# Tokens on partitions for values, gates and branch products: 512 weight columns a product, weight parts in pairs

## The chip, the core and the metric

The kernel runs on one core of a Trainium2 chip, in one launch. The metric is the device time in microseconds. The engines are named as the profile names them: PE (matrix products), PEld (its weight loads), ACT, DVE, POOL, and SP, which here only issues DMAs. The program is built with a scheduler: the code gives the instructions a priority, and the scheduler puts them into one fixed order for each engine. Each engine then runs its queue in that order, and an instruction that waits holds up all that stand behind it.

## The reference, cut to what matters

Two layers, 256 tokens, 1024 features, float32. `_mixer` projects the normalized input onto the columns of `w_in`, runs two recurrences on parts of them, and merges the two results under gates; `_conv_ffn` follows.

```python
x = x + W_out( sig(h Wg_dn) * (DeltaNet_bi(h) W_dn) + sig(h Wg_hg) * (HGRN2_bi(h) W_hg) ),  h = RMSNorm(x)
x = x + ConvGLU(RMSNorm(x))

p = h @ w_in
(qkv, z, beta_r, a_r, hq, hf_fwd, hf_bwd, hi, hgate, gate_dn, gate_hg) = _split(p, IN_SIZES)
...
o_dn = _gated_rmsnorm(o_dn, z...)          # o * rsqrt(mean(o^2)) * w * silu(z)
o_hg = _gated_rmsnorm(o_hg, hgate...)
merged = (jax.nn.sigmoid(gate_dn) * (o_dn @ w_branch_dn)
          + jax.nn.sigmoid(gate_hg) * (o_hg @ w_branch_hg))
return merged @ w_out
...
gate = _dwconv(gate, ffn_conv) + ffn_conv_bias
return (jax.nn.silu(gate) * up) @ w_down
```

## The kernel before, in words

**Products.** Most matrix products are made three times over in the type fp32r. A weight piece (128 x 1024 values: four blocks of 128 rows by 256 columns) arrives by DMA as `raw`; ACT casts it to `wh`, DVE subtracts to get the remainder `wl`; the activations have parts `xh` and `xl` in the same way. A product is then `wh*xh + wh*xl + wl*xh`, summed in a PSUM bank (`Gemm`, lines 208 to 244). The pools hold three `raw`, three `wh` and three `wl` (each one piece). Some projections skip the split and multiply plain float32 (`gemm32`, line 249): numbers 1, 4, 5, 6 and 14 of `w_in`, and 2 and 3 ahead of the mixer (`Pre`).

**Layout.** Nearly every product has a 128 x 128 block of weights as the stationary operand and 256 tokens as the moving one, so the result has channels on partitions. For z, the HGRN2 gate (projections 14 to 17, `silu_gate`) and the HGRN2 values (9 and 13, `hi_`) it is turned round with `tokens=True`: a 128 x 128 block of activations is stationary, and 256 weight columns move. The gates (18 to 25, `gates`) and the branch products (`branches`, line 913) keep channels on partitions.

**A mixer.** After its first projections it builds the DeltaNet system (`gram`, `solve`, `inverse`, `delta`) and the two HGRN2 halves (`hgrn`, two heads at a time, result `poh`). Then `out_norm` normalizes each half's output: `ob` (copy), `junk` (squares on ACT), `rr` (root), `on` on DVE, four or two transposes `pto` on PE, and `ohl`, the two parts, on ACT and DVE. `branches` multiplies `ohl` by the branch weights (bank `pbr`), multiplies by the sigmoid gates `sgt`, adds the two branches (`mg`) and splits the sum into `mhi` and `mlo`; `project` multiplies those by `w_out`. The gate projections depend on nothing late, so they stand in PE's queue beside the chains of the recurrences.

**Order.** The strings `"order"` in `OPT`, one for each layer, list the stages (`k0` conv, `z0` gate, `hi0` values, `g0` gates, `hg1` HGRN2, `ho1` its output, `br`, `pr`) with a priority offset each; weight splits stand 2000 ahead of their users (`"ahead"`). The feed-forward part (`ffn`, line 975) is a loop over 22 blocks of 256 columns of `w_up`, and four column blocks of `w_down`.

Of the kernel before, what the change touches and what calls it, by code (L numbers as in the profile page):

```python
# [17 lines left out]
P = 128  # L18
T = 256
# [9 lines left out]
    "f32": ((1, 4, 5, 6, 14), (1, 4, 5, 6, 14)),  # L29
# [6 lines left out]
    "w": 3,  # L36
    "rp": 20000,
    "eu": 0,
# [5 lines left out]
    "es": ((), ()),  # L44
    "ec": 1,
    "eo": 0,
# [13 lines left out]
    "tmz": 1,  # L60
# [15 lines left out]
# columns of the per-layer vector pack (one value per partition each)  # L76
# [11 lines left out]
# columns of the constants  # L88
# [28 lines left out]
def trunk(ctx: ExitStack, tc: tile.TileContext, x_in, consts, masks, vec, rows, w16, w_in, w_br, w_out, w_up, w_down, out):  # L117
# [21 lines left out]
    class Group:  # L139
        """Matmuls accumulating in one PSUM bank, kept in order; one start, one stop."""  # L140
# [9 lines left out]
    # ---------------------------------------------------------------- constants  # L150
# [32 lines left out]
    # ---------------------------------------------------------------- helpers  # L183
# [8 lines left out]
    def split_piece(src, n):  # L192
        with tc.high_priority(offset=OPT["ahead"]):
            return split_piece_(src, n)

    def split_piece_(src, n, pool=None, bufs=0):
        raw = piece(src, n)
        if pool:
            wh = pool.tile([P, 1024], F32R, tag="eh", name="wh", bufs=bufs)
            wl = pool.tile([P, 1024], F32R, tag="el", name="wl", bufs=bufs)  # L200
        else:
            wh = wp.tile([P, 1024], F32R, tag="wh", name="wh", bufs=OPT["w"])
            wl = wp.tile([P, 1024], F32R, tag="wl", name="wl", bufs=OPT["w"])
        act.copy(wh[:, :n], raw[:, :n])  # L204
        dve.tensor_tensor(wl[:, :n], raw[:, :n], wh.bitcast(F32)[:, :n], ALU.subtract)  # L205
        return (wh[:, :n].rearrange("p (k c) -> p k c", c=256), wl[:, :n].rearrange("p (k c) -> p k c", c=256))

    class Gemm:
        """src[i]: [P, k, 256] pieces; fills a bank: two column tiles (T layout) or two token tiles."""

        def __init__(self, src, xh, xl, nk=KT, tokens=False, tail=0, parts=None):
            self.tail, self.parts = tail, parts
            self.src, self.xh, self.xl, self.nk, self.tokens = src, xh, xl, nk, tokens
            self.ps = pg.tile([P, 512], F32, tag="g", name="ps", bufs=OPT["g"])
            self.g = Group(nk * 6)
            self.k = 0

        def run(self, k1=None):
            nk = k1 or self.nk
            while self.k < nk:  # L220
                last = self.nk - self.k <= 4 * self.tail
                end = nk if last else min(self.k + 4, nk)
                w = []
                for k0 in range(self.k, end, 4):
                    kn = min(4, end - k0)
# [20 lines left out]
    def gemm(src, xh, xl, nk=KT, tokens=False, tail=0, parts=None):  # L246
        return Gemm(src, xh, xl, nk, tokens, tail, parts).run()
# [950 lines left out]
```

## Time and profile before

| what | value |
|---|---|
| median of three runs | 928.67 us (927.70 to 929.71) |
| span of the profiled execution | 926.8 us, 1.9 us under the median, which lies around the span |
| PE busy | 906.6 us, 98% of the span, 7450 instructions |
| DVE busy | 668.5 us, 72% |
| ACT busy | 559.0 us, 60% |
| DMA | 150.07 MB, mean 162 GB/s |
| granted TensorE clock | 0.998 in the mean |

The page's 40 slices are 23.2 us each. The mixer of layer 0 fills the first eleven, its feed-forward part the next nine; layer 1 repeats this from about 470 us. The profile times one execution; its span runs from the first to the last instruction, and the device time has the start and end of the launch on top. In the timeline a row with `x4` stands for four instructions in a row, and starts of neighbouring rows show the pace of PE better than the durations, because products overlap in the array.

### The profile page before, as it was taken

The page shows a single profiled execution, that of the slowest core. Times are in us where ns is not written, and L with a number is a line of the kernel's source. Part 1 is how long each engine was busy: PE and PEld are TensorE (multiplying, and loading weights), DVE is VectorE, ACT ScalarE, POOL GpSimd, SP SyncE. Part 2 cuts the span into 40 slices and gives each one's busy share as a digit, 9 for nine tenths or more (in the row PEclk, how much of TensorE's full clock was granted, in tenths as well). Part 3 has the DMA queues.
Part 4 walks back from the last instruction along what each step waited for, and adds up shares of the span by engine and source line. Part 5 has one row for each costly group of instructions (what it writes and reads, how often), then busy time and mean ns, then how long its engine had stood idle before and what let it go on. Part 6 is the DMA issues. An engine that isn't in the chain of part 4 may idle for free.

```text
span 926.8 us, 18732 instructions
## 1 busy us (share of the span) xinstructions
PE 906.6 (98%) x7450; PEld 887.8 (96%) x7450; DVE 668.5 (72%) x1279; ACT 559.0 (60%) x974; POOL 13.9 (2%) x123
## 2 busy tenths in 40 slices
PE   7999999999999999999999999999999999999997
PEld 6988999999999999999989899999999999999996
DVE  4667997655877888865447889885667788888543
ACT  4698647678566555543437856665855665555443
POOL 0000000000000000000000000000000000000000
PEclk9999999999999999999999999999999999999999
DMA  6455554225567655555505564533265656555552
GB/s 207 137 189 169 171 184 124 69 74 177 183 202 250 186 183 183 183 176 174 171 27 170 183 205 149 152 100 92 91 197 175 192 184 187 183 183 183 171 183 80
DMA packets 51111, 150.07 MB, mean 162 GB/s; under 512 B 13488, under 2 KB 14032, under 8 KB 50768
## 3 DMA queue, kind: packets, MB, share of 16 engines
q1 hardware_dynamic: 50304, 147.96, 50.5%
q8 instruction: 58, 0.95, 0.4%
q10 hardware_dynamic: 720, 0.92, 0.3%
q14 instruction: 29, 0.24, 0.1%
HBM read 146.75 MB, written 2.11 MB: 161 GB/s over the span
## 4 chain that ended last, share of the span: by engine, by line
PE 88%; ACT 4%; DMA 3%; DVE 3%; issue 1%; SPq 0%; DVEq 0%; ACTq 0%
PE ps L146 72%; PE pbr L146 5%; PE pa L830 3%; DMA raw<-in_w_in_dram 2%; DVE wl L205 1%; DMA ld<-dg 1%; PE po L146 1%; PE poh L146 1%; PE psb L146 1%; ACT wh L204 1%; PE ss L146 0%; PE pz L666 0%; PE pr L689 0%; DMA xs<-in_consts_dram 0%; DVE pr L627 0%
## 5 line engine op out<-in xcount | busy, mean ns | idle before, releaser
L204 ACT CAST wh<-raw 128x1024 fp32r<-128x1024 f32 x244 | 251.8, 1035 | 250.7 <-PE ps L146 96.0
L205 DVE TENSOR_TENSOR wl<-raw,wh 128x1024 fp32r<-128x1024 f32 x244 | 293.6, 1205 | 127.1 <-ACT wh L204 123.7
L146 PE MATMUL ps<-xh,wl 128*128 128x256 f32 x1152 | 327.2, 285 | 1.5 <-DVE wl L205 1.5
L146 PE MATMUL ps<-xh,wh 128*128 128x256 f32 x1152 | 327.1, 285 | 1.2 <-ACT wh L204 1.2
L146 PE MATMUL ps<-xl,wh 128*128 128x256 f32 x1152 | 326.2, 284 | 0.0
L146 PEld LDWEIGHTS ps<-xh,wl 128*128 128x128 f32 x1152 | 220.1, 192 | 2.3 <-DVE wl L205 2.1
L146 PEld LDWEIGHTS ps<-xh,wh 128*128 128x128 f32 x1152 | 220.3, 192 | 1.7 <-ACT wh L204 1.4
L146 PEld LDWEIGHTS ps<-xl,wh 128*128 128x128 f32 x1152 | 220.3, 192 | 0.1
L146 PE MATMUL ps<-hl,wh 128*128 128x256 f32 x352 | 99.0, 281 | 0.0
L146 PE MATMUL ps<-hh,wl 128*128 128x256 f32 x352 | 99.0, 281 | 0.0
L146 PE MATMUL ps<-hh,wh 128*128 128x256 f32 x352 | 98.6, 280 | 0.0
L146 PEld LDWEIGHTS ps<-hh,wl 128*128 128x128 f32 x352 | 66.3, 188 | 0.1
L146 PEld LDWEIGHTS ps<-hl,wh 128*128 128x128 f32 x352 | 66.3, 188 | 0.1
L146 PEld LDWEIGHTS ps<-hh,wh 128*128 128x128 f32 x352 | 66.3, 188 | 0.0
L146 PE MATMUL ps<-xnt,raw 128*128 128x256 f32 x256 | 58.8, 380 | 0.0
L146 PEld LDWEIGHTS ps<-xnt,raw 128*128 128x128 f32 x256 | 47.0, 190 | 6.0
L146 PE MATMUL ps<-wl,xh 128*128 128x256 f32 x160 | 47.1, 294 | 0.7 <-DVE wl L205 0.6
L146 PE MATMUL ps<-wh,xh 128*128 128x256 f32 x160 | 46.6, 292 | 0.2 <-ACT wh L204 0.2
L146 PE MATMUL ps<-wh,xl 128*128 128x256 f32 x160 | 46.1, 288 | 0.0
L1001 DVE SCALAR_TENSOR_TENSOR cv<-fpad,vecs,cv 128x256 f32<-128x256 f32 x88 | 42.2, 480 | 4.3
L146 PE MATMUL pbr<-ohl,wh 128*128 128x256 f32 x256 | 45.3, 280 | 0.0
L146 PEld LDWEIGHTS pbr<-ohl,wh 128*128 128x128 f32 x256 | 38.8, 188 | 0.0
(274 smaller groups left out, 1438.1 us busy)
## 6 DMA issues: line engine op xcount, KB each, us to landing
raw<-in_w_in_dram SPq DMA_DIRECT2D x99, 512.0 KB, 3.6
raw<-in_w_up_dram SPq DMA_DIRECT2D x88, 512.0 KB, 3.7
raw<-in_w_down_dram SPq DMA_DIRECT2D x40, 512.0 KB, 3.6
raw<-in_w_br_dram SPq DMA_DIRECT2D x16, 512.0 KB, 3.9
raw<-in_w_out_dram SPq DMA_DIRECT2D x16, 512.0 KB, 4.2
cb<-cd SPq DMA_DIRECT2D x2, 1024.0 KB, 5.6
early<-in_w_in_dram SPq DMA_DIRECT2D x4, 512.0 KB, 7.2
raw<-in_w_down_dram SPq DMA_DIRECT2D x8, 256.0 KB, 3.3
```

The source lines that it names most:

```text
L146: self.prev = chain(pe.matmul(o, lhsT, rhs, start=self.i == 0, stop=self.i == self.n - 1), self.prev)
L204: act.copy(wh[:, :n], raw[:, :n])
L205: dve.tensor_tensor(wl[:, :n], raw[:, :n], wh.bitcast(F32)[:, :n], ALU.subtract)
L830: pe.matmul(pa[:, u // 2, u % 2], kc[:, u * P:(u + 1) * P], view(qa[:, 0, u * P:u * P + 1], [[2 * h, 64 // h], [512 + h, 2], [1, h]]), sta ...
L1001: dve.scalar_tensor_tensor(cv, pad[:, i:i + T], w[:, i:i + 1], cv, op0=ALU.mult, op1=ALU.add)
```

## The change: what it does

1. **Tokens on partitions, 512 columns.** A new `gemm_tok` makes products with a 128 x 128 block of activations stationary and 512 weight columns moving (two pieces side by side, 256 columns of each), into two banks `pst`, one for each block of 128 tokens. z and the HGRN2 gate, the values, the gates and the branch products all use it.
2. **Pairs.** `split_pair` brings two pieces into one tile `w2`, which holds both parts of both; there are two such tiles, where there were three `wh` and three `wl`. All other split products, the feed-forward part's too, take their weights from pairs.
3. **Projection 14** is no longer plain float32.
4. **Merge.** The gated branch results are summed as [token, 512 columns]; PE transposes the sum (`ptm`, four blocks of 128 columns each), and the two parts are split out of that bank into `mg2`, whose first half lies in the buffer `xw` and whose second in `cb`. For each layer there are 8 multiplications and 4 additions of 512 columns, 16 transposes and 4 splits of 512, in place of 8 multiplications of 512, 8 additions and 8 splits of 256.
5. **Names and order.** `qk` lies in the buffer `xw`. The order strings join stages (`hi0` and `hi1` to `hi`, `z0` to `z3` to two, `g0` to `g7` to four) and keep the offsets. Options that were off are removed.

```diff
-    "f32": ((1, 4, 5, 6, 14), (1, 4, 5, 6, 14)),
+    "f32": ((1, 4, 5, 6), (1, 4, 5, 6)),
...
-    "w": 3,
+    "w": 2,
...
-        "g0-5000 hf1-1000 hb1-300 hg1-2000 z2-2000 z3-1000 do-300 g1-300 ho0-1000 g2-3000 ho1 g3 g4-1000 "
-        "g5-1000 g6-9000 g7 br-9000 pr-1000",
+        "g0-5000 hf1-1000 hb1-300 hg1-2000 z1-2000 do-300 g1-300 ho0-1000 g2-3000 ho1 g3 br-9000 pr-1000",
...
-    def split_piece(src, n):
+    def split_pair(srcs, ns=(1024, 1024)):
+
         with tc.high_priority(offset=OPT["ahead"]):
...
+            w2 = wp.tile([P, 2, 2, 1024], F32R, tag="w2", name="w2", bufs=OPT["w"])
+            for i, (src, n) in enumerate(zip(srcs, ns)):
+                raw = piece(src, n)
+                split_act(raw[:, :n], w2[:, 0, i, :n], w2[:, 1, i, :n])
+            return w2
...
+    def gemm_tok(src, xh, xl):
+
+
+        n = len(xh)
+        ps = [pg.tile([P, 512], F32, tag="g", name="pst", bufs=OPT["g"]) for _ in range(2)]
+        gs = [Group(3 * n) for _ in range(2)]
+        for i in range(n // 4):
+            w2 = split_pair([src(i, j) for j in range(2)])
+            for b in range(2):
+                o = ps[b].rearrange("p (j c) -> p j c", j=2)
+                for k in range(4):
+                    wh, wl = (w2[:, e, :, 256 * k:256 * k + 256] for e in range(2))
+                    a, a_ = (t_[4 * i + k][:, b * P:(b + 1) * P] for t_ in (xh, xl))
+                    gs[b].mm(o, a, wh)
+                    gs[b].mm(o, a, wl)
+                    gs[b].mm(o, a_, wh)
+        return ps
...
-            qk = mp.tile([P, 2, H, T], F32, tag="qk", name="qk")
+            qk = xp.tile([P, 2, H, T], F32, tag="xw", name="qk")
...
             def gates(c):
-                j, t0 = divmod(c, 4)
+                j, t0 = divmod(c, 2)
...
+                for b, ps in enumerate(win_tok(18 + 2 * c)):
+                    act.activation(sgs[0][:, b, j, 512 * t0:512 * t0 + 512], ps, AF.Sigmoid)
...
+            def silu_gate(i):
+                sz.append(mp.tile([P, 2, 512], F32, tag=("t1", "ke")[i], name="sz"))
+                for b, ps in enumerate(win_tok(14 + 2 * i)):
...
+            def hi_():
+                iv = late().tile([P, 2, 512], F32, tag="iv", name="iv")
+                for b, ps in enumerate(win_tok(9, 13)):
+                    act.copy(iv[:, b], ps)
...
+                for c in range(2):
+                    m_ = (xp, mp)[c].tile([P, 2, 4, T], F32R, tag=("xw", "cb")[c], name="mg2")
+                    tms = []
                     for i in range(2):
...
+                        for b, ps in enumerate(gemm_tok(lambda _, j: w_br[l, 2 * c + j, i], oh[i], ol[i])):
+                            tm = tmp("mg", ("tmp", "tmh")[i])
+                            dve.tensor_tensor(tm, ps, sgs[0][:, b, i, 512 * c:512 * c + 512], ALU.mult)
+                            tms.append(tm)
+                    for b in range(2):
+                        dve.tensor_tensor(tms[b], tms[b], tms[2 + b], ALU.add)
+                        pt = bank("ptm")
+                        for k in range(4):
+                            pe.transpose(pt[:, k], tms[b][:, k * P:(k + 1) * P], ident)
+                        split_act(pt, m_[:, 0, :, b * P:(b + 1) * P], m_[:, 1, :, b * P:(b + 1) * P])
```

How the instructions stand on the engines is shown at three places, all in layer 0. In the rows of the changed kernel `w_2252` and the like are the pair tiles `w2`, and `mg_2249` is a half of `mg2`.

PE, at the first z products (projection 14), before: `raw` is the unsplit weight piece and `xnt` the activations in float32.

```order
L146 MATMUL ps<-xl,wh 128x256
L146 MATMUL ps<-xh,wl 128x256
L146 MATMUL ps<-xh,wh 128x256
L146 MATMUL ps<-xl,wh 128x256
L146 MATMUL ps<-xh,wl 128x256
L146 MATMUL ps<-raw,xnt 128x256 x7
L600 MATMUL gram<-qk 128x128 x2
L146 MATMUL ps<-raw,xnt 128x256
L530 MATMUL qtr<-cst,qk 128x128 x4
```

The same place in the changed kernel; `w_881` and `w_947` are the last pairs of the two forget-gate projections, and `w_1302` is the first pair of z.

```order
L139 MATMUL ps<-xh,w_881 128x256
L139 MATMUL ps<-xh,w_947 128x256
L139 MATMUL ps<-xl,w_881 128x256
L139 MATMUL ps<-xl,w_947 128x256
L139 MATMUL ps<-xh,w_881 128x256
L139 MATMUL ps<-xh,w_947 128x256
L139 MATMUL pst<-w_1302,xh 128x512 x2
L139 MATMUL pst<-w_1302,xl 128x512
L139 MATMUL pst<-w_1302,xh 128x512 x2
L139 MATMUL pst<-w_1302,xl 128x512
```

The z products took the unsplit `raw` before. Now they need both parts of both pieces of a pair, and stand right behind two projections that end one product apart.

PE, from the last branch products to the output projection, before.

```order
L146 MATMUL pbr<-ohl,wl 128x256
L146 MATMUL pbr<-ohl,wh 128x256 x2
L146 MATMUL pbr<-ohl,wl 128x256
L146 MATMUL ps<-mhi,wh 128x256
L146 MATMUL ps<-mlo,wh 128x256
L146 MATMUL ps<-mhi,wl 128x256
L146 MATMUL ps<-mhi,wh 128x256
```

The same place in the changed kernel; `w_2291`, `w_2347` and `w_2386` are pairs of branch weights, `w_2446` and `w_2510` the first two pairs of `w_out`.

```order
L139 MATMUL pst<-w_2291,ohl 128x512 x6
L869 MATMUL pto<-cst,on 128x128 x2
L139 MATMUL pst<-w_2347,ohl 128x512 x12
L139 MATMUL pst<-w_2291,ohl 128x512 x6
L902 MATMUL ptm<-cst,mg 128x128 x4
L139 MATMUL pst<-w_2386,ohl 128x512 x24
L902 MATMUL ptm<-cst,mg 128x128 x12
L139 MATMUL ps<-mg_2249,w_2446 128x256
L139 MATMUL ps<-mg_2249,w_2510 128x256
L139 MATMUL ps<-mg_2249,w_2446 128x256 x23
```

Twelve transposes `ptm` now stand between the last branch product and the first output projection.

ACT at that place, before: `wh` is a weight cast, `mhi` the high part of the merge.

```order
L204 CAST wh<-raw 128x1024
L266 CAST mhi<-mg 128x256
L204 CAST wh<-raw 128x1024
L266 CAST mhi<-mg 128x256
L204 CAST wh<-raw 128x1024 x2
L279 ACTIVATE sa<-x_81 128x512
```

ACT in the changed kernel; `w_2510` is the second pair of `w_out`, `mg_2249` and `mg_2344` the two halves of `mg2`.

```order
L255 CAST w_2386<-raw 128x1024 x2
L255 CAST w_2446<-raw 128x1024
L255 CAST mg_2249<-ptm 128x4x128
L255 CAST w_2446<-raw 128x1024
L255 CAST w_2510<-raw 128x1024 x2
L255 CAST mg_2249<-ptm 128x4x128
L255 CAST mg_2344<-ptm 128x4x128 x2
L255 CAST w_2576<-raw 128x1024 x2
```

The merge casts, which stood one by one between single weight casts, now stand behind the two casts of a pair, three of the four together.

## Rows read from the trace of the kernel before

**Rows 1.** Page: span; busy time by engine; DVE and TensorE clock by fortieth of span.

```profile
span 926.8 us, 18732 instructions
...
PE 906.6 (98%) x7450; PEld 887.8 (96%) x7450; DVE 668.5 (72%) x1279; ACT 559.0 (60%) x974; POOL 13.9 (2%) x123
...
DVE  4667997655877888865447889885667788888543
...
PEclk9999999999999999999999999999999999999999
```

**Rows 2.** Waits of PE, the two longest: engine, line, releaser: us, times, longest.

```profile
PE ps L146 <- DMA raw<-in_w_in_dram: 5.7, 1, 5.7
PE ps L146 <- DVE wl L205: 2.1, 3, 1.3
```

**Rows 3.** Timeline of PE at 300 us: start, us, engine, line, operation, count.

```profile
299.74 0.28 PE L146 MATMUL ps<-xl,wh 128*128 128x256 f32 x1
...
301.18 0.28 PE L146 MATMUL ps<-xl,wh 128*128 128x256 f32 x1
```

**Rows 4.** Timeline of PE, layer 0, last branch products and first output projection.

```profile
248.26 0.63 PE L146 MATMUL pbr<-ohl,wh 128*128 128x256 f32 x4
248.73 0.40 PE L146 MATMUL pbr<-ohl,wl 128*128 128x256 f32 x2
...
250.97 0.28 PE L146 MATMUL pbr<-ohl,wl 128*128 128x256 f32 x1
251.09 0.28 PE L146 MATMUL ps<-mhi,wh 128*128 128x256 f32 x1
```

**Rows 5.** Timeline of PE, layer 1, plain float32 products, two records each.

```profile
473.21 7.07 PE L146 MATMUL ps<-xw,early 128*128 128x256 f32 x32
480.12 3.64 PE L146 MATMUL psb<-wb,xw 128*128 128x16 f32 x32
```

**Rows 6.** Groups by shape, PE: projection 14 in both layers; busy us, mean ns.

```profile
L146 PE MATMUL ps<-raw,xnt 128*128 128x256 f32 x64 | 14.9, 379 | 0.0
```

**Rows 7.** Timeline of PE, layer 1, last HGRN2 outputs and first transposes.

```profile
653.27 1.73 PE L146 MATMUL poh<-iv,at 128*128 128x128 f32 x14
654.84 0.49 PE L895 MATMUL pto<-cst,on 128*128 128x128 f32 x3
```

**Rows 8.** Groups by shape, DVE: weight low parts, branch merge, low parts from a bank.

```profile
L205 DVE TENSOR_TENSOR wl<-raw,wh 128x1024 fp32r<-128x1024 f32 x236 | 288.0, 1222 | 117.5 <-ACT wh L204 114.1 <-PE ps L146 2.4
...
L933 DVE TENSOR_TENSOR mg<-pbr,sgt 128x512 f32<-128x512 f32 x16 | 10.5, 685 | 0.6 <-PE pbr L146 0.6
...
L934 DVE TENSOR_TENSOR mg<-mg 128x256 f32<-128x256 f32 x16 | 6.7, 416 | 0.0
...
L898 DVE SCALAR_TENSOR_TENSOR ohl<-pto,vecs,ohl 128x512 fp32r<-128x512 f32 x4 | 3.0, 750 | 2.5 <-ACT ohl L897 2.5
```

**Rows 9.** Groups by shape, ACT: weight casts, casts from a bank.

```profile
L204 ACT CAST wh<-raw 128x1024 fp32r<-128x1024 f32 x236 | 246.8, 1049 | 235.5 <-issue 91.5 <-PE ps L146 83.7 <-DMA raw<-in_w_in_dram 21.6
...
L897 ACT ACTIVATE ohl<-pto,vecs 128x512 fp32r<-128x512 f32 x4 | 2.8, 689 | 0.0
```

**Rows 10.** Windows: HGRN2 tails, layer 0's branches; length, then busy us of PE, PEld, DVE, ACT.

```profile
197.00:226.00 29.00, 29.00 (x247) 29.00 (x247) 18.35 (x38) 26.31 (x56) 0.00 (x0) 1.00 0.41 128
226.00:251.00 25.00, 25.00 (x215) 25.00 (x214) 18.83 (x29) 12.20 (x17) 0.00 (x0) 1.00 0.58 184
655.00:684.00 29.00, 29.00 (x245) 29.00 (x244) 17.84 (x32) 20.94 (x39) 0.00 (x0) 1.00 0.52 161
```

**Rows 11.** Timeline of PE and DVE: last poh of layer 0, last ohl of both layers.

```profile
197.15 0.39 PE L146 MATMUL poh<-iv,at 128*128 128x128 f32 x2
...
228.08 0.48 DVE L898 SCALAR_TENSOR_TENSOR ohl<-pto,vecs,ohl 128x256 fp32r<-128x256 f32 x1
...
676.45 0.48 DVE L898 SCALAR_TENSOR_TENSOR ohl<-pto,vecs,ohl 128x256 fp32r<-128x256 f32 x1
```

**Rows 12.** Timeline of PE, layer 0, the wait nearest to the first z products.

```profile
77.93 0.39 PE L146 MATMUL ps<-xh,wl 128*128 128x256 f32 x1 [1.25 <-DVE wl L205]
```

More of the change, by code (lines that the diff above doesn't have):

```diff
@@ L59 @@
     "tmh": 3,
-    "tmz": 1,
     "g": 3,
@@ L218, in run @@
[L218 to L225, printed above, removed]
-                    wh, wl = self.parts[k0 // 4] if self.parts else split_piece(self.src(k0 // 4), kn * 256)
-                    w += [(wh[:, kk], wl[:, kk]) for kk in range(kn)]
-                ks = range(self.k, end)
+        def run(self):
+            for k0 in range(0, self.nk, 8):
+                ks = range(k0, min(k0 + 8, self.nk))
+                at = [i for i in (0, 4) if k0 + i < self.nk]
+                w2 = split_pair([self.src((k0 + i) // 4) for i in at], [256 * min(4, self.nk - k0 - i) for i in at])
+                last = self.nk - k0 <= 8 and self.tail
@@ L243, in run, with gemm @@
-                self.k = end
-            return self.ps
-    def gemm(src, xh, xl, nk=KT, tokens=False, tail=0, parts=None):
-        return Gemm(src, xh, xl, nk, tokens, tail, parts).run()
-    def gemm32(src, xw, tokens=False):
+                    wh, wl = w2[:, 0, i, c:c + P], w2[:, 1, i, c:c + P]
+                    self.g.mm(o, wh, a)
+                    self.g.mm(o, wh, b)
+                    self.g.mm(o, wl, a)
+            return self.ps
+    def gemm(src, xh, xl, nk=KT, tail=0):
+        return Gemm(src, xh, xl, nk, tail).run()
@@ L340, in __init__ @@
             self.g = [Group(KT * 2) for _ in PRE]
-            self.parts, self.stack = {}, None
             self.last = None
-        def ahead(self, l):
-            if not OPT["es"][l]:
-                return
-            self.stack = ExitStack()
-            pool = self.stack.enter_context(tc.tile_pool(name=f"ep{l}", bufs=1, side="right", reuse_waits=OPT["rw"]))
-            n = 2 * len(OPT["es"][l])
-            with tc.high_priority(offset=OPT["eo"]):
-                for c in OPT["es"][l]:
-                    self.parts[c] = [split_piece_(w_in[l, c, i], 1024, pool, n) for i in range(2)]
         def add(self, c):
@@ L796, in hf @@
                     act.activation(kb[:, d, s], sn[:, s], AF.Identity, scale=oms[:, l, c:c + 1])
[L798 to L801 removed]
+            def hi_():
+                iv = late().tile([P, 2, 512], F32, tag="iv", name="iv")
+                for b, ps in enumerate(win_tok(9, 13)):
+                    act.copy(iv[:, b], ps)
+                for e in range(2):
+                    hg["i", e] = iv[:, :, 256 * e:256 * e + 256]
             def hgrn(e):
@@ L944, in project @@
                 for c in range(4):
-                    if c == 3 and OPT["eu"]:
-                        up.run(4)
                     ps = gemm(lambda i: w_out[l, c, i], mh, ml)
@@ L957, in mixer @@
                 stages[("q0", "q1", "v0", "v1")[i]] = lambda c=c: conv(c)
-            for i in range(8):
+            stages["hi"] = hi_
+            for i in range(4):
                 stages[f"g{i}"] = lambda i=i: gates(i)
-            for i in range(4):
+            for i in range(2):
                 stages[f"z{i}"] = lambda i=i: silu_gate(i)
@@ L1016, in ffn @@
                         pre.mm(todo[:OPT["ek"]])
-                if c == OPT["ec"] and not last:
-                    pre.ahead(l + 1)
                 gm = Gemm(lambda i: w_down[l, c, i] if i < 5 else w_down[l, c, i][:, 0:512], hh, hl, NF,
@@ L1057, in trunk @@
     pre.mm(todo[:OPT["e0"]])
-    pre.ahead(0)
     rs, rm = meet(pre, rs, todo[OPT["e0"]:], OPT["fa0"])
```

107 lines of the change are left out of this document (22 added, 85 removed), and 9 rows, old and new, of the table OPT.

## The prediction, made before the changed kernel ran

> **What bounds the kernel now.** I read the page first. PE is busy 906.6 us of a span of 926.8 us, while DVE is busy 72% and ACT 60%, and the TensorE clock is granted in full in every slice [rows 1]. The reader should see that only 20 us of the span are not PE, so an edit that gives PE no less work and lets it wait no longer gains nothing. The waits come second: the longest is the first weight transfer, 5.7 us, which the change doesn't touch; the next in size are 2.1 us for weight low parts (`wl`) in three pieces [rows 2]. The kernel is bound by the number of products and their pace, and the change acts on that pace. Third come windows, because a busy PE hides how full the others are beside it: in the HGRN2 tail of layer 0 ACT is busy 26.31 us of 29, in layer 1's 20.94 of 29, and PE 29.00 in both [rows 10]. There the filler (gate and branch products, in PE's queue beside the chain of `out_norm`) is what keeps PE busy. Less PE time for that filler is a gain only as far as the chain is shorter than the filler.
>
> **Pace of a product.** Twelve starts of split products lie 1.44 us apart, 120 ns each for 256 columns [rows 3]; branch products run at (248.73 - 248.26) / 4 = 117.5 ns [rows 4]. No row shows a split product of 512 columns. Two rows bound it. A float32 product of 256 columns is recorded as two passes, each 512 column steps by its time: 32 records from 473.21 to 480.12 are 216 ns each [rows 5]. That is the low end. The high end is twice the row for 256 columns, 240 ns. I take 216: at 128 columns the float32 outputs start every (654.84 - 653.27) / 14 = 112 ns [rows 7], close to the 117.5 to 120 of 256 columns, so by these rows a product of 256 pays mostly for something that doesn't grow with columns, as a load of 128 stationary columns would. A product of 512 columns would hide that.
>
> The Trainium skill, "TensorE: Matmul & The Clock Gate", Back-to-back issue gap, speaks against the change: it gives the gap as N / 2.4 + 2.5 ns at full clock, so 109.2 ns at 256 columns and 215.8 at 512, and joining two products would save only 2.6 ns. Its value for 512 agrees with the row of 216; for 256 the trace shows 117.5 to 120, and the measurement decides. By the rule's two figures the saving below would be near 2 us in place of 18.5, an estimate from that page.
>
> **What PE saves, for each layer.** Gates: 8 projections of 48 products, 384 x 0.120 = 46.1 us, become 192 x 0.216 = 41.5: 4.6 saved. z and the HGRN2 gate: 144 x 0.120 plus projection 14 with 32 records (64 in both layers [rows 6]) x 0.216 = 24.2, become 96 x 0.216 = 20.7: 3.5. Values: 96 x 0.120 = 11.5, become 48 x 0.216 = 10.4: 1.1. Branches: 192 x 0.1175 = 22.6, become 96 x 0.216 = 20.7: 1.8. Against this 16 transposes of the merge, 16 x 0.112 = 1.8 [rows 7]. The sum is 9.2 us for a layer, 18.5 for both.
>
> **What it adds beside PE.** Projection 14 now needs two more casts (1.05 us each [rows 9]) and two more subtractions (1.22 each [rows 8]) for each layer. DVE's `wl` stood idle 117.5 us before its starts, almost all of it because ACT's cast came late or the buffer was not free [rows 8]; I cost them at nothing, and at 2 x 2.4 = 4.9 us if that room isn't where they fall. The merge swaps 8 additions of 0.416 for 4 of about 0.685 (the 512-column row) and 8 small splits for 4 of at most 0.75 on DVE and 0.69 on ACT [rows 8, 9]: about even. The moved buffer of `qk` and the joined stages issue no new work. The pairs hold as many bytes as four single buffers of each part did (before: three). In the feed-forward loops a pair lasts 48 x 0.120 = 5.76 us on PE, and the next-but-one needs two casts and a subtraction after its buffer is free: 1.05 + 1.22 + 1.22 = 3.5. The other pair's products hide it with 2.3 us in hand, so I cost it at nothing; each 0.1 us missed over some 44 pairs of up and 24 of down would be 6.8 us.
>
> **New waits.** Three places lose their cover.
>
> *Start of the output projection, both layers.* Before, `mhi` came in small steps and the first `w_out` product starts 0.12 us after the last `pbr` [rows 4]. Now the last bank must be multiplied (0.69) and added (0.69), then transposed, then split. On ACT the third `mg2` cast stands behind the two casts of a `w_out` pair, which wait for the pair tile that the last branch product frees: 2 x 1.05, then the merge cast of about 0.5, ends 2.6 us after that product. On DVE the low part stands behind two subtractions and ends near 4.5 us. PE has 12 transposes (8 of them at once, 0.9 us) and two products before it needs the low part. The wait is 4.5 - 1.5 = 3.0 us, 6.0 for both layers. Zero would need the merge casts ahead of the pair, which the order rules out.
>
> *First z products, layer 0.* Projection 14 took `raw`, with no split. Now two forget-gate projections, one product apart, free both pair tiles at the same moment, and the z pair needs two casts and two subtractions from there: 3.5 us, less one product, 3.3. The wait of 1.25 us for a low part near there [rows 12] goes. Net 2.0. In layer 1 I see the same kind of place but with other products near; 0 to 3.3, taken 0.
>
> *The tails.* From the last `poh` at 197.15 to the last `ohl` in layer 0 it is 228.56 - 197.15 = 31.4 us, in layer 1 676.93 - 654.7 = 22.2 (the last of 14 `poh` starts at 653.27 + 13 x 0.112) [rows 7, 11]. By the order of the changed kernel PE has between the same two points in layer 0 76 products of 512, ten `pto` and seven `poh`: 76 x 0.216 + 17 x 0.112 = 18.3 us, in layer 1 69 products and eight `pto`: 15.9 with two `poh`. If the chain takes as long as it did, PE waits 13.1 and 6.3 us; if the chain only took what PE happened to give it, nothing. Layer 1's 22.2 us shows that 31.4 isn't the chain's need, so I take 22.2 - 18.3 = 3.9 for layer 0, and half of 6.3, 3.2, for layer 1, whose casts are in the way only part of the time (ACT 20.94 of 29 [rows 10]). Together 7.1, between 0 and 19.4.
>
> **Sum.** Waits 6.0 + 2.0 + 7.1 = 15.1. The profiled span of 926.8 lies 1.9 us under the median of 928.7, and I carry that rest unchanged: span 926.8 - 18.5 + 15.1 = 923.4, time 925.3. I forecast 925.
>
> **Rivals.**
> 1. *The chains fit* (faster, 914). ACT and DVE follow the shorter filler, as in the windows where they were full and PE did not wait [rows 10]. Then only the project starts remain: 928.7 - 18.5 + 6.0 - 1.3 = 914.9. Against it: 26.31 of 29 us on ACT in layer 0 leave it little to give.
> 2. *The tail becomes the bound* (slower, 938). The chain from `poh` to the last `ohl` takes 31.4 and 22.2 us as now, since pair casts (2.1 us at a time) stand between its steps on ACT. The tails cost 19.4 in place of 7.1: 925.3 + 12.3 = 937.6. It decides for slower as soon as both tails wait over 10.5 us together. For it: ACT's share in layer 0, and that a paired cast holds up a step of the chain twice as long. Against it: layer 1 shows that the chain can be faster.
> 3. *512 columns cost twice 256* (slower, 942). At 240 ns the gates, values and branches gain nothing, z gains 24.2 - 23.0 = 1.2, the transposes cost 1.8: 0.6 lost for a layer, 1.3 in all. Starts and z cost 8.0, the tails with a longer filler (20.1 and 17.6) 2.1 and 2.3: 928.7 + 1.3 + 12.4 = 942.4. Against it: rows 5. The page's rule above would land near it too, since it leaves little saving.
> 4. *The change doesn't do what it says* is excluded: the order shows the 512-column products.
>
> **How the numbers follow.** My forecast has a chance of 0.48, with its own range of 919 to 930; rival 1 has 0.15, rival 2 0.30, rival 3 0.07. A difference under 0.2% (1.9 us, about what a measurement of this kernel can tell) is the same, so faster is below 926.8 and slower above 930.5. Of the forecast's 0.48 I put 0.34 below, 0.09 between, 0.05 above. Rival 1 is all faster. Rival 2 reaches down to no change with 0.02, and below it with 0.01; the rest and rival 3 are slower. Faster 0.50, same 0.11, slower 0.39. The range: 909 takes in rival 1 with nothing left of the waits but 0 at z and part of the project starts; 940 takes in rival 2 with the DVE pieces half uncovered. Rival 3 and the outer ends are left out, under 0.2.
>
> **What would show it.** Starts of `pst` products 216 ns apart show the pace right; 235 or more, rival 3. PE's busy time should fall by about 18 us and its waits rise by about 15. `ps <- mg2` waits of about 3 us at the start of each output projection, `pst` waiting near 3 us for a low part at layer 0's z, and waits of `pst` and `pto` for `ohl` and `on` in both tails are the terms of the sum; no waits there is rival 1, over 10.5 us in the tails rival 2. Waits in the up or down loops would show the cover of the pairs wrong, and would make the prediction wrong by some 7 us for each 0.1.

## The result, and the profile after

The changed kernel takes 971.21 us in the median (970.78 to 975.29, four runs) against 928.28 us (927.7 to 929.71): a ratio of 1.0469, interval 1.0448 to 1.049. It is slower by 43 us, where 3 us faster was forecast. The profiled execution took 975.29 us, 4 us over the median.

The head of the page after, and longer waits of PE; they answer to [rows 1] and [rows 2].

```profile
span 973.2 us, 16999 instructions
...
PE 922.9 (95%) x6650; PEld 855.7 (88%) x6650; DVE 668.1 (69%) x1267; ACT 551.9 (57%) x966; POOL 13.9 (1%) x123
...
PEclk9999899999999999999999999999988999999998
```

```profile
PE pst L139 <- DVE w L256: 11.8, 11, 4.6
PE pst L139 <- ACT w L255: 8.4, 7, 3.8
PE ps L139 <- DMA raw<-in_w_in_dram: 7.1, 2, 6.2
PE ps L139 <- DVE mg L256: 3.7, 2, 2.4
PE pst L139 <- ACT ohl L871: 3.7, 4, 1.6
...
PE pto L869 <- DVE on L867: 1.4, 2, 1.0
```

Two things are new: some 20 us of waits of 512-column products for their weights, and a clock that is not granted in full. PE is busy 16.3 us longer, not 18 us shorter. The next rows, 4 us windows of layer 0 (length, PE, PEld, DVE, ACT, POOL, then the granted clock, DMA share, GB/s), show why both belong together.

```profile
100.00:104.00 4.00, 0.61 (x2) 0.52 (x3) 3.93 (x8) 3.99 (x9) 0.00 (x0) 0.59 0.25 49
104.00:108.00 4.00, 4.00 (x12) 3.17 (x11) 3.90 (x11) 3.06 (x6) 0.00 (x0) 0.56 0.84 327
108.00:112.00 4.00, 4.00 (x19) 3.32 (x18) 3.76 (x9) 2.24 (x4) 0.00 (x0) 1.00 0.34 126
```

PE was busy 0.6 us of 4, and in the 4 us behind that it makes 12 products, at a granted clock of 0.56, where it makes 19 once the clock is back. The clock record of the kernel after lists nine stretches at 1.2 GHz before its last products, where the one before lists none. PE is busy in them for 32.6 us, of which half, 16.3 us, is lost. The part of the span in which PE isn't busy grew from 20.2 to 50.3 us. 30.1 and 16.3 are the whole difference of the spans, 46.4: PE's work at full clock did not shrink (922.9 - 16.3 = 906.6 busy, as before).

Where it went, by stages marked by their first and last products (`gram`, the last `poh` of each HGRN2 half, the first and last `w_out` product; layer 1's down ends with PE's last transpose), in us:

| stage | layer 0 before | after | layer 1 before | after |
|---|---|---|---|---|
| to the first `gram` | 55.6 | 57.3 | 45.8 | 45.2 |
| to the first half's last `poh` | 97.7 | 108.5 | 91.0 | 99.5 |
| to the second half's last `poh` | 48.3 | 63.7 | 49.3 | 76.6 |
| to the first `w_out` product | 49.4 | 37.0 | 49.5 | 37.5 |
| output projection | 22.3 | 25.1 | 22.3 | 26.9 |
| up | 128.1 | 128.1 | 128.1 | 128.1 |
| down | 67.1 | 67.5 | 66.1 | 66.1 |

The windows of layer 0 (as above; from the first `gram` on, and then by the same marks) before and after:

```profile
55.60:153.30 97.70, 93.88 (x768) 90.44 (x768) 79.45 (x185) 71.69 (x132) 2.76 (x2) 1.00 0.58 179
153.30:201.70 48.40, 48.40 (x485) 47.45 (x485) 30.45 (x62) 32.53 (x71) 0.00 (x0) 1.00 0.21 67
201.70:251.10 49.40, 49.40 (x420) 49.40 (x419) 35.58 (x59) 33.88 (x57) 0.00 (x0) 1.00 0.53 168
```

```profile
57.30:165.80 108.50, 98.95 (x715) 87.79 (x716) 84.27 (x189) 72.28 (x137) 2.77 (x2) 0.97 0.50 156
165.80:229.50 63.70, 63.70 (x418) 56.30 (x417) 41.93 (x78) 45.98 (x85) 0.00 (x0) 1.00 0.38 121
229.50:266.50 37.00, 31.73 (x135) 23.50 (x133) 23.88 (x37) 20.77 (x38) 0.27 (x6) 0.95 0.42 134
```

And layer 1 after, the last two of these stretches:

```profile
632.00:708.50 76.50, 75.20 (x534) 65.50 (x533) 46.78 (x85) 46.11 (x90) 0.00 (x0) 1.00 0.34 108
708.50:746.00 37.50, 31.72 (x122) 23.03 (x122) 19.78 (x32) 16.73 (x34) 0.00 (x0) 0.86 0.31 98
```

The stretch of the second HGRN2 half is longer and has next to no idle time (none, and 1.3 us): PE does gate products there that it did later before. The trace shows it by count: behind the last `poh` stood 208 products of 256 columns on `xh` and `xl` in each layer before, as many as 104 of 512, and 10 and 4 stand there now. The tail behind it is 12 us shorter, and now it has idle time and a lower clock. The work moved forward, past the chain that it should have run beside.

The tails aren't all of it. Idle time of PE and half-clock losses together, over the kernel before: 18.2 us from the first `gram` to the first half's last `poh` in both layers (12.8 idle, 5.4 clock), 17.1 in the tails (11.1 and 6.0), 6.9 in the output projections, 4.2 elsewhere.

The pace: a run of 512-column products of the gates, and one of the branches (PE's timeline after, as in [rows 3]).

```profile
205.07 0.39 PE L139 MATMUL pst<-w,xl 128*128 128x512 f32 x1
205.30 0.62 PE L139 MATMUL pst<-w,xh 128*128 128x512 f32 x2
...
206.43 0.39 PE L139 MATMUL pst<-w,xl 128*128 128x512 f32 x1
...
231.22 2.73 PE L139 MATMUL pst<-w,ohl 128*128 128x512 f32 x11
233.78 0.62 PE L139 MATMUL pst<-w,xh 128*128 128x512 f32 x2
```

Six products in 206.43 - 205.07 us are 227 ns each, eleven in 2.56 us 233. Two products of 256 columns took 240 and 235 [rows 3, 4].

### The profile page after: what moved, and what is told of

The parts are those of the page before. It is cut to its first block, busy times and chain, and to the rows that moved or that the text cites. A ratio compares the mean times of both kernels' runs of the same rounds, so it can differ in the third digit from the quotient of the medians.

```text
span 973.2 us, 16999 instructions
## 1 busy us (share of the span) xinstructions
PE 922.9 (95%) x6650; PEld 855.7 (88%) x6650; DVE 668.1 (69%) x1267; ACT 551.9 (57%) x966; POOL 13.9 (1%) x123
## 4 chain that ended last, share of the span: by engine, by line
PE 81%; DVE 7%; DMA 5%; ACT 4%; issue 2%; SPq 0%; DVEq 0%; ACTq 0%
PE ps L139 53%; PE pst L139 18%; DVE w L256 3%; PE pa L804 2%; DMA raw<-in_w_in_dram 2%; ACT w L255 1%; DMA xs<-in_consts_dram 1%; PE poh L139 1%; PE po L139 1%; PE psb L139 1%; DMA cb<-cd 1%; DVE xs L605 1%; DVE pr L603 1%; DMA ti<-xd 1%; DVE np__257 L579 0%
## 5 line engine op out<-in xcount | busy, mean ns | idle before, releaser
L256 DVE TENSOR_TENSOR w<-raw,w 128x1024 fp32r<-128x1024 f32 x248 | 292.3, 1203 | 98.9 <-ACT w L255 97.9
L255 ACT CAST w<-raw 128x1024 fp32r<-128x1024 f32 x248 | 248.1, 1035 | 192.3 <-PE ps L139 112.9
L139 PE MATMUL ps<-xh,w 128*128 128x256 f32 x1792 | 327.2, 284 | 1.1 <-DVE w L256 1.1
L139 PEld LDWEIGHTS ps<-xh,w 128*128 128x128 f32 x1792 | 280.0, 192 | 1.9 <-DVE w L256 1.3
L139 PE MATMUL ps<-xl,w 128*128 128x256 f32 x896 | 252.3, 283 | 0.0
L139 PEld LDWEIGHTS ps<-xl,w 128*128 128x128 f32 x896 | 171.1, 192 | 0.3
L139 PE MATMUL pst<-w,xh 128*128 128x512 f32 x448 | 152.5, 412 | 16.4 <-DVE w L256 8.9
L139 PE MATMUL ps<-hh,w 128*128 128x256 f32 x704 | 125.5, 281 | 0.0
L139 PEld LDWEIGHTS ps<-hh,w 128*128 128x128 f32 x704 | 108.1, 188 | 0.1
L139 PE MATMUL ps<-hl,w 128*128 128x256 f32 x352 | 99.0, 281 | 0.0
L139 PE MATMUL pst<-w,ohl 128*128 128x512 f32 x192 | 55.6, 438 | 8.5 <-ACT ohl L871 3.7
```

Of the source, the lines that this page charges most:

```text
L139: self.prev = chain(pe.matmul(o, lhsT, rhs, start=self.i == 0, stop=self.i == self.n - 1), self.prev)
L255: act.copy(hi, src)
L256: dve.tensor_tensor(lo, src, hi.bitcast(F32), ALU.subtract)
```

## The experiments

Each is told beside its runs of the kernel before, whose median was 928.2 to 929.5 us in every set.

**Pairs alone.** The kernel before, with pairs and its own order; `qk` and `mhi` in `xw` for room.

```diff
-    "w": 3,
+    "w": 2,
...
+            w2 = wp.tile([P, 2, 2, 1024], F32R, tag="w2", name="w2", bufs=OPT["w"])
...
-            qk = mp.tile([P, 2, H, T], F32, tag="qk", name="qk")
+            qk = xp.tile([P, 2, H, T], F32, tag="xw", name="qk")
...
-                mhi = mp.tile([P, KT, T], F32R, tag="qk", name="mhi")
+                mhi = xp.tile([P, KT, T], F32R, tag="xw", name="mhi")
```

> The kernel before, with its 128x256 products and its order, but every weight split in pairs of pieces in two pair tiles (qk and mhi moved to the buffer xw to make room, as the changed kernel does). Theory P (the loss comes from the pairs: two tiles that come free together, and nothing is ready until four casts or subtractions are done): 950 to 968 us, with waits of products for casts and low parts in the mixers of 10 us or more. Rival Q (the loss comes from the products of 512 columns and the shorter filler they leave, pairs cost nothing): 925 to 935.

966.78 us, ratio 1.0417 (1.038 to 1.0454). Theory P as it seemed. But up and down took 128.1 and 67.5 us in layer 0, against 128.1 and 67.1 before: where nothing but one loop runs, pairs cost next to nothing. And the run holds a second edit: moving `qk` and `mhi` alone gave 948.29 us, as told below, so 18.5 us are left for the pairs and the order that they bring.

**512 columns with single pieces.** The changed kernel; a piece for a 512-column product is two row blocks by 512 columns.

```diff
-    "w": 2,
+    "w": 3,
...
-            w2 = split_pair([src(i, j) for j in range(2)])
...
+            w = split([(src(i // 2, j)[:, 512 * (i % 2):512 * (i % 2) + 512], 512) for j in range(2)])
```

> The changed kernel with its products of 512 columns, its merge and its order, but weights split one piece at a time in three wh and three wl, as before: a piece for a 512-column product is two blocks of 128 rows by 512 columns, so each piece still feeds 12 such products. Theory P: most of the loss goes, 920 to 940, waits for weights under 8 us. Rival Q: 955 to 972, the waits stay. A product pace of 227 to 234 ns stays in either.

937.77 us, 1.009 (1.0057 to 1.0123). Most of the loss is gone with the pairs, and 9 us stay.

**Splits further ahead.**

```diff
-    "ahead": 2000,
+    "ahead": 9000,
```

> The changed kernel with the weight splits standing 9000 in place of 2000 ahead of their users in the scheduler's priorities. If the waits come from casts that stand behind other ACT and DVE work which was ready too (theory R: the old priorities no longer fit), 945 to 962; if they come from the pair tiles coming free too late or from chains that the filler no longer covers, 966 to 978.

972.83 us, 1.0462 (1.043 to 1.0493): theory R, in this form, falls.

**Values and HGRN2 gate alone.** The kernel before; `qk` and `mhi` stand in `xw` here too, and the stages `hi1` and `z3` are gone from the order.

```diff
...
-                act.copy(iv.rearrange("p a b -> p (a b)"), win(9 + 4 * e, tokens=True))
...
+                for b, ps in enumerate(win_tok(9, 13)):
+                    act.copy(iv[:, b], ps)
```

> The kernel before with single pieces, where only the values (9, 13) and the HGRN2 gate (16, 17) are products of 512 columns (pieces of two blocks of rows by 512 columns); projections 14 and 15, gates, branches and merge as before. By the pace read in the changed kernel, 48 pairs of products a layer gain 13 ns each for each of the two: 2 x 96 x 0.013 = 2.5 us faster, 925 to 928, if 512 columns do no harm by themselves (theory P). Rival Q: 930 or more, because a unit takes two of the three banks.

936.01 us, 1.0082 (1.005 to 1.0114). No gain, though it has neither pairs nor gates at 512. This shook both theories.

The next four asked what a small edit costs by itself.

> The kernel of single pieces with 512-column products (937.8), with four wh and four wl in place of three: the same bytes as the two pair tiles of the changed kernel. If what hurt with pairs is that weights come free and are made ready in large lots, not how many bytes there are (theory P), 928 to 940, far under 971. If more room ahead is what the 512-column kernel lacked, 920 to 930.

967.44 us, 1.0417 (1.0385 to 1.045), for one more buffer of each part (`"w": 4`). More room made it slower by 30 us. This is the run that killed theory P as I had put it: it has no pairs. Its stages look like those of the changed kernel: 63.3 us to the second half's last `poh` in layer 0, and a tail of 37.9.

> The kernel before, with only qk and the merge's high parts moved to the buffer xw, which the runs with pairs and with 512-column values also had. If the move is free, 927 to 930, and the 8 us of the run with 512-column values and HGRN2 gate belong to the 512-column units; if the move makes qk wait for the readers of xw or changes the order for the worse, 932 to 938, and those units are cleared.

948.29 us, 1.0208 (1.0176 to 1.0239), for two lines that move `qk` and `mhi`. In layer 1 the stages from the first `gram` took 89.6, 49.3 and 49.5 us, about as before (91.0, 49.3 and 49.5); nearly all of the loss is in layer 0. There 34 more plain float32 records and 48 more products of 256 columns with tokens on partitions stand ahead of the first `gram` than before, which came at 72.0 us in place of 55.6.

> The kernel before with two wh and two wl in place of three, single pieces. If the number of tiles decides (two users at a time leave none free to be made ready ahead), 950 to 985, as with two pairs; if the size of a lot decides, 928 to 940.

949.7 us, 1.0229 (1.0199 to 1.0259): in neither range, 0.3 us under the first. Here the waits for weights in up and down are seen too (down 69.3 and 70.3 us).

> The kernel with 512-column products, single pieces and four of each part, with the stage of the values (now all four heads at once) placed behind the first queries and forget gates instead of ahead of them. In the run with three of each, the stretch up to the first Gram product took 58.5 us against 55.6. If that is the joined values standing too early, 3 us of it come back in each layer against the run with four of each and the old place; if not, the two are equal within 2 us.

957.65 us, 1.0308 (1.0281 to 1.0336): 10 us from the run it varies, by the place of one stage. The first stretch fell from 59.1 to 56.9 and from 49.2 to 43.0 us, as expected, but 91.3 us then went to the second half in layer 0, behind which a tail of 30.3 was left.

Two of these, four buffers with the values at either place, share with the changed kernel a short tail and a long time. The other two, `qk` moved and two single tiles, keep tails of 49.5 to 55.5 us and are slower all the same, so a short tail can't be the reason there. **Theory S**, formed here: the edits let the scheduler take gate products earlier, in front of the HGRN2 chain, and what is then left beside the end of that chain is too little. I counted the work behind the last `poh` in the order of each kernel, and put it to the test on both sides.

**The kernel before, with the order of the changed one's gate stages.**

```diff
...
-        "g0-5000 hf1-1000 hb1-300 hg1-2000 z2-2000 z3-1000 do-300 g1-300 ho0-1000 g2-3000 ho1 g3 g4-1000 "
-        "g5-1000 g6-9000 g7 br-9000 pr-1000",
+        "g0-5000 g1-5000 hf1-1000 hb1-300 hg1-2000 z2-2000 z3-1000 do-300 g2-300 g3-300 ho0-1000 g4-3000 g5-3000 "
+        "ho1 g6 g7 br-9000 pr-1000",
...
```

Layer 1's order changes in the same way.

> The kernel before, its instructions and buffers untouched, with only the gate stages' places and offsets as the changed kernel's joined stages have them (g0 and g1 at 5000, g2 and g3 at 300, g4 and g5 at 3000 or 2000 ahead of the last out_norm stage, g6 and g7 at 0). By the order the work after the last HGRN2 output falls from 49.9 and 49.9 to 19.7 and 29.6 us. Theory S: 945 to 970, with the same kinds of wait as the changed kernel (for ohl, on and the merge) and low clock in the tails. Theory P: 927 to 932, since it has neither pairs nor 512 columns.

955.92 us, 1.0287 (1.0267 to 1.0307). Theory S holds: 26 us by nothing but the place of the gates. Its windows in layer 0, between the same marks:

```profile
56.30:159.60 103.30, 98.57 (x857) 94.50 (x856) 80.86 (x186) 71.32 (x132) 2.76 (x2) 1.00 0.53 169
159.60:236.40 76.80, 74.56 (x649) 73.58 (x648) 44.95 (x80) 48.92 (x89) 0.00 (x0) 1.00 0.36 116
236.40:268.00 31.60, 24.33 (x168) 23.07 (x167) 18.84 (x39) 15.02 (x34) 0.00 (x0) 0.84 0.26 85
```

The same picture as after the change: the second half ends late with PE busy nearly all the way (2.2 us idle), then a short tail with 7.3 us idle and a clock of 0.84. The longest waits are of the same kind:

```profile
PE pto L895 <- DVE on L893: 7.0, 3, 3.7
```

**The changed kernel with other priorities.**

```diff
...
-        "g0-5000 hf1-1000 hb1-300 hg1-2000 z1-2000 do-300 g1-300 ho0-1000 g2-3000 ho1 g3 br-9000 pr-1000",
...
+        "... g0-300 hf1-1000 hb1-300 hg1-9000 z1 do-300 g1 ho0-9000 g2 ho1-9000 g3 br-9000 pr-1000",
...
```

Layer 1's order changes in the same way.

> The changed kernel, its instructions untouched, with other priorities alone: the four joined gate stages at 300, 0, 0, 0 (were 5000, 300, 3000 or 2000, 0), the second HGRN2 half, both out_norm stages of it at 9000, the HGRN2 gate at 0. By the order, counted at the paces read, the PE work after the last HGRN2 output and before the output projection grows from 28.5 and 26.1 us (layers 0 and 1; 49.9 in the kernel before) to 43.1 and 50.5. Theory S (the old offsets, on joined stages, pull gate products ahead of the HGRN2 chain; the chain ends later and its tail has too little left beside it): 935 to 955, waits for ohl and mg2 nearly gone. Theory P (the pairs themselves): 965 to 975.

955.35 us, 1.0273 (1.0236 to 1.031): 16 us back, and 0.35 us over the range of theory S. Layer 0 by the same marks:

```profile
56.40:160.00 103.60, 91.92 (x606) 82.14 (x607) 80.83 (x185) 68.02 (x130) 2.76 (x2) 0.93 0.51 163
160.00:214.00 54.00, 54.00 (x438) 48.08 (x438) 32.42 (x59) 34.09 (x63) 0.00 (x0) 1.00 0.22 69
214.00:258.00 44.00, 41.98 (x195) 33.66 (x193) 29.54 (x51) 34.03 (x64) 0.00 (x0) 1.00 0.47 155
```

The tail is healed (2.0 us idle, full clock). The first stretch is not: 11.7 us idle and a clock of 0.93, and 7.4 us idle in layer 1.

**Single pieces, two other orders.** Gates at 0; and with the second HGRN2 half and its `out_norm` at 9000.

> The kernel of 512-column products with single pieces (three of each part; 937.8), with the four gate stages at offset 0 and nothing else changed. Work after the last HGRN2 output by the order: 47.6 and 51.6 us, as in the kernel before; it was 51.2 and 45.7. Theory S: 928 to 938, no worse than it was; if 512-column units by themselves hold back the chain, 937 to 945.

935.31 us, 1.0075 (1.0049 to 1.01).

> As the run before last (512 columns, single pieces, gates at 0), with the second HGRN2 half and its out_norm at 9000 as well: 54.9 and 56.4 us of work after the last HGRN2 output. Theory S: within 6 us of that run, 925 to 938; the saving of the pace (about 8 us) would show here if anywhere.

937.22 us, 1.0088 (1.0055 to 1.0122). The tails idle 0.0 and 0.6 us in the first, 0.3 and 2.8 in the second, yet neither is faster than before. With a mended tail on either side, pairs cost 18 to 20 us (955.35 against 937.22 and 935.31; the order strings are near, not the same) and 512 columns with single pieces 6 to 8. The traces show where most of it sits: from the first `gram` to the first half's end PE idles 19.1 us with pairs and 7.7 with single pieces and gates at 0, both layers together, and loses 6.6 and 3.3 us there to the clock.

**What the 20 us are: both pieces before the first product?** The pair's two pieces become row halves.

```diff
...
+                for j, src in enumerate(srcs):
+                    sp.dma_start(raw[:, 512 * j:512 * j + 512], src[:, 512 * i:512 * i + 512])
...
```

> The changed kernel with the priorities of the run after_order (955.4), and one more edit: the two pieces of a pair for a 512-column product are two blocks of rows by 512 columns each, in place of four blocks of rows by 256 columns each, so the first product needs one cast and one subtraction instead of two and two. Tiles, bytes, casts and subtractions stay. Theory U (a 512-column product waits for both pieces of a pair, and that is the rest of the loss, 17 us of waits of pst for casts and low parts): 935 to 945. Rival V (both pair tiles come free at the same moment, whatever lies in them): 950 to 960, the waits stay.

954.71 us, 1.0282 (1.0251 to 1.0312). Waits of `pst` for casts and low parts fell from 17.2 to 5.4 us, as theory U has it, but the time stayed. That doesn't refute theory U in the first stretch: PE's idle time there fell from 19.1 to 13.5 us and its clock loss from 6.6 to 2.2, while tails and output projections, with the same order strings, now idle 9.1 us in place of 2.4 and lose 5.1 to the clock in place of none. What was won in front was lost behind. In front, a wait of 4.3 us for a low part now stands at another product in the same place. Its rows, on PE and on DVE, show what is late.

```profile
94.25 0.79 PE L135 MATMUL ps<-xh,w 128*128 128x256 f32 x2 [4.34 <-DVE w L262]
```

```profile
91.61 0.20 DVE L609 TENSOR_TENSOR pr<-lm,xs 128x31 f32<-128x31 f32 x1 [5.38 <-DMA xs<-in_consts_dram]
...
92.97 1.22 DVE L262 TENSOR_TENSOR w<-raw,w 128x1024 fp32r<-128x1024 f32 x1
```

DVE's queue holds the first step of `solve`, which waits 5.4 us for the constants `xs`, and the subtractions that PE needs stand behind it. In the kernel after it is the same queue, with 5.9 us on DVE and the 4.6 us of its longest wait on PE:

```profile
103.39 0.80 PE L139 MATMUL pst<-w,xh 128*128 128x512 f32 x1 [4.60 <-DVE w L256]
```

```profile
95.06 0.21 DVE L603 TENSOR_TENSOR pr<-lm,xs 128x31 f32<-128x31 f32 x1 [5.92 <-DMA xs<-in_consts_dram]
...
100.79 1.22 DVE L256 TENSOR_TENSOR w<-raw,w 128x1024 fp32r<-128x1024 f32 x1
```

There the wait for `xs` was over before ACT began the pair's casts at 96.25; what held the subtraction until 100.79 was the run of `solve` steps that the wait had put back. Before, DVE waited at most 2.8 us there.

**Projection 14 back in float32**, with pairs and with single pieces.

```diff
...
+                ps = gemm(src, xh, xl, tokens=True) if j else gemm32(src, xn, True)
...
```

> The kernel after_order (pairs, 955.4) with projections 14 and 15 as in the kernel before: 14 plain float32 from the unsplit piece, 15 a product of 256 columns, each its own stage at its old place. The rest of the order string stays, but the scheduler then leaves 19.4 us of work after the last HGRN2 output in layer 0 (43.1 in after_order) and 48.8 in layer 1 (50.5), so layer 1 is the one to read. Theory W (projection 14 in float32 was the work that needed neither cast nor subtraction while DVE waits for the constants of the solve and ACT is busy): from the first Gram product to the end of the first HGRN2 half in layer 1, PE's idle time falls from 7.4 us to 4 or less and no wait over 2 us for a weight is left there. Rival V (the pair tiles): it stays at 6 or more.

961.54 us, 1.036 (1.0335 to 1.0385). In layer 1, from the first `gram` to the first half's end, idle time fell from 7.4 to 5.5 us, one wait of 3.1 us for a cast is left, and the stretch took 104.5 us in place of 97.5. Between the two bounds: theory W isn't shown.

> The kernel of 512-column products with single pieces, with projections 14 and 15 as in the kernel before, gates at 0 and behind the second HGRN2 half, that half and its out_norm stages at 9000: 47.6 and 54.4 us of work after the last HGRN2 output. Theory W with theory S: 926 to 934, the best of the 512-column kernels (935 so far). If the loss lies with the order as a whole and not with projection 14, 934 to 945.

934.56 us, 1.0062 (1.0045 to 1.0078): the lowest median of the 512-column kernels, though not clear of 935.31, at a clock of 0.996 and with no wait over 1.5 us but the first transfer's, and still slower than before. Its split products on `xh` and `xl` and its branch products (each from its start to the next start, or to its own end where PE idles behind it) take 521.7 us, those of the kernel before 531.0; the products' pace does save 9 us there. The transposes of the merge (3.3), HGRN2's `pa` (3.0), plain float32 (2.7), `w_out` (1.3) and idle time between products (3.9) take it back and more.

**Values and HGRN2 gate alone, two orders**, `qk` in its old place.

> The kernel before with 512 columns for the values and the HGRN2 gate alone, single pieces, qk in its old place (the buffer of the gate's sigmoid shared to make room), gates g0 and g2 at 1000 and 0, the second HGRN2 half at 9000: 51.2 and 51.0 us of work after the last HGRN2 output by the order. The pace would gain 2.4 us. If the order is as good as the old one, 925 to 928; the earlier run of this kind gave 936. If the old string was simply better fitted than any that a count of filler finds, 930 to 938.

938.71 us, 1.0116 (1.0076 to 1.0155).

> As the run with values and HGRN2 gate before it, with other offsets: gates as in the kernel before, the second HGRN2 half at 9000 and its out_norm stages at 5000; 45.4 and 52.0 us of work after the last HGRN2 output by the order. 925 to 928 or 930 to 938, as there; the distance of the two shows how far equal instructions differ by their order alone.

938.73 us, 1.0101 (1.008 to 1.0122). Two orders chosen by the count of filler, the same time, both 10 us slower: a full tail isn't enough. The stretch up to the first half's end took 105.5 and 108.0 us in layer 0 against 97.7, but the next ones gave most of that back: from the first `gram` to the output projection layer 0 took 198.4 and 198.6 us against 195.4, and layer 1 196.8 and 197.0 against 189.8. No version here beats the kernel before.

## Why the prediction was wrong, by its own steps

By the terms of its sum, the prediction put the span at 923.4 us, and 973.2 was measured. PE's work was to shrink by 18.5 us and did not shrink: 18.5. PE's time without work was to grow by 15.1 us and grew by 30.1: 15.0. The clock stood in no term: 16.3. These make up the 49.8 us. The steps behind them:

- **The pace** was the first term mis-sized. I took 216 ns for 512 columns from the float32 row; 227 to 234 was measured. With these paces the four sums for a layer give 2.5 for gates, 2.4 for z, 0.6 for values and 0.1 for branches, less 1.8 for transposes: 7.7 us for both layers in place of 18.5. What a product pays beyond its columns is the same at both widths: 120 - 106.7 = 13 ns, 227 - 213.3 = 14 ns. My reading, that a load of the stationary block explains it and is hidden by 512 columns, falls. The row that it rested on was misread: a float32 product is recorded twice at 128 columns too (16 `poh` records for 8 products in each half), so by the count of [rows 5] one record of 112 ns is 256 column steps, not 128, and 112 beside 117.5 to 120 shows no cost that stays when the columns halve. The Trainium skill's rule ("TensorE: Matmul & The Clock Gate", Back-to-back issue gap), which that section gives for an isolated product, a fixed part added to N / 2.4, spoke against the change and had the form right; its 2.5 ns is not what these rows show. The measured pace lies between mine and rival 3's 240. Even the 7.7 us can't be seen in PE's busy time at full clock: in the trace the products that changed form took 8.6 us less, and the transposes `ptm` and `pto` 6.3 and plain float32 1.7 more.
- **The wait in the tails.** The prediction counted what stands behind the last `poh` (18.3 and 15.9 us up to the last `ohl`, [rows 11]) and priced it as a wait there, 7.1 us. Up to that point PE idled 2.4 and 4.9 us, 7.3 together, so the number came out, in part by luck. In layer 0 of the kernel before, the row at 197.15 is only the first of its group; the last `poh` is the last of the fourteen in the row below and starts at 201.69. The chain took 26.9 us there and not 31.4, and after the change it took 21.0 and 27.0.

```profile
200.24 1.73 PE L146 MATMUL poh<-iv,at 128*128 128x128 f32 x14
```

- **The place of the filler** is the step that failed there. The prediction took the PE work ahead of that point as unchanged, and never asked where the missing filler had gone. It had gone in front: counted from the start of their layers, the second halves end 28 and 35 us later than before (1.7 + 10.8 + 15.4; 8.5 + 27.3 - 0.6), and only 12 us of that return as a shorter tail. Joined stages with kept offsets did it: `g0-5000` now carries two gates' work in one. The order rows I quoted began at the branches; the stretch that decided lay ahead of them. The run of the kernel before with those offsets shows 26 us for it, and the changed kernel with others gives 16 back; the two need not be equal, since what the tail misses differs.
- **Rival 2** had the sign, 938, and the wrong place for most of it: the tail's own idle time is 5.3 and 5.8 us up to the output projection, not 19.4.
- **First z products, layer 0.** Priced at 3.3 us; 2.0 and 4.6 us were measured, of which the longer one waits for DVE, held by `solve` as shown above. The queue of DVE at that place was not read.
- **Layer 1's z** was taken at 0; 7.5 us of waits of `pst` for weights lie between 500 and 640 us. From the first `gram` to the first half's end the two layers together idle 12.8 us more than before, where the sum had a net 2.0: the largest of its waits that was mis-sized, and the one that the new priorities did not touch.
- **Start of the output projection.** 3.0 us a layer forecast; 4.5 us of waits of `ps` for `mg2` in both layers together, and the stage is 2.8 and 4.6 us longer, 3.2 of it clock. Right in kind.
- **Pairs in up and down** cost nothing, as forecast: 128.1 us each time.
- **The clock** was not in the sum at all. The stretches at half clock, eight of nine in or shortly behind waits, cost a second time: 16.3 us, a third of the loss.

What stays open: how the 18 to 20 us of the pairs with a mended tail divide. They lie mostly in the waits for weights before the first half's end and in the clock there. The wait behind `solve` is part of it and was seen with and without whole pairs; that a pair in place of two pieces moves the order, and how much of the 20 is that, was not separated. Nor was the merge tried by itself, which is part of the 6 to 8 us of the 512-column kernels with single pieces, nor was it settled why moving `qk` alone reorders layer 0 and not layer 1. Three pair tiles could not be tried, for want of room.

## What to carry to other kernels

Where a scheduler orders the queues from priorities, an edit that joins stages or changes a buffer count is also an edit of the order, and here that was worth more (26 us for the gates' offsets alone) than the change itself could bring (under 10). Before pricing such a change, count the independent work on the bound engine in each stretch between the marks of the long chain, before and after, not only in the stretch with the waits: work that is missing at the end has been spent in front of the chain. Count idle time too, and in every stretch: the edit that mended the waits in front here brought new ones behind. Whether it helps to keep a product at hand that needs nothing from the helpers, as projection 14 was, these runs don't show.

## What the runs showed of the hardware that was not expected

A product of 512 columns with 128 stationary columns takes 227 to 234 ns at full clock, one of 256 columns 117 to 120. PE's clock went to half in nine stretches of the changed kernel and in none of the kernel before, whose longest wait after the start is 1.25 us [rows 12]. In or shortly ahead of eight of them PE had waited between products (by up to 4.6 us); the ninth, at 503 us, follows 32 products of 16 columns (`psb`) with no wait, and the kernel before makes the same ones at full clock, so waits alone don't account for it. Three more runs have such a stretch behind the same products (splits further ahead, single pieces, single pieces with gates at 0), the others none. At half clock 512 columns took 0.43 us, as the first two of these rows of PE's timeline after show; the other two are the products at the ninth stretch.

```profile
103.98 0.63 PE L139 MATMUL pst<-w,xl 128*128 128x512 f32 x1
104.41 1.06 PE L139 MATMUL pst<-w,xh 128*128 128x512 f32 x2
...
499.13 3.64 PE L139 MATMUL psb<-wb,xw 128*128 128x16 f32 x32
502.62 3.79 PE L139 MATMUL ps<-xnt,raw 128*128 128x256 f32 x10
```
